# One more couple by seven products, a weight combination made on the fly, and an input tile sent alone

## The chip, the cores and the metric

The kernel runs on one core of a Trainium2 chip. The metric is the device time of one execution in microseconds (us); smaller is better. A kernel is run several times and the median is given, with the lowest and highest run beside it. One execution of each kernel is also recorded by the hardware profiler; its span is the time from the first to the last instruction recorded.

The engines of the core are TensorE (PE in the profile: matrix products into the PSUM banks; PEld is its weight load), VectorE (DVE), ScalarE (ACT), GpSimd (POOL) and SyncE (SP), which here issues most transfers (DMAs). Each engine runs its own instructions in order and waits for the others by semaphores.

## The reference

A trunk of two layers on 256 tokens of width 2048, all in fp32. Each layer has a token mixer (mLSTM in the first, HGRN2 in the second) and a gated feed-forward part, both added to the stream; a norm closes it. What matters here is the feed-forward part, and of it the second product:

```python
def conv_glu(hn, w_up, conv_w, conv_b, w_down):
    u = hn @ w_up
    a, v = jnp.split(u, 2, axis=-1)
    ...
    return (jax.nn.gelu(c, approximate=False) * v) @ w_down

for layer in range(DEPTH):
    ...
    h = h + mix
    h = h + conv_glu(rmsnorm(h, norm_ffn_g[layer]), ffn_w_up[layer], ...)
return rmsnorm(h, final_g)
```

`w_down` is 5504 x 2048 in each layer.

## The kernel before

**Products.** Each fp32 operand is split into a high part (rounded, for PE) and a low part (what is left). A product of two operands is three matmuls: high x high, high x low, low x high. `product` (L236) issues the three. For weights, `parts` (L141 to L149) makes the split: ACT casts the high part `wh` (L147), DVE subtracts and leaves `wl` (L148). This is done for every piece of 128x1024 or 128x512 numbers that PE uses, just ahead of it; six pieces can be in flight.

**Stages.** A list of chunks runs through PE one after the other: the mLSTM mixer, the feed-forward of layer 0, the HGRN2 mixer, the feed-forward of layer 1. A feed-forward part is worked in two halves of its 5504 inner columns, 22 and 21 tiles of 128. Each half first computes its up tiles (each ended by `done_up`, from L1187: the gate, the convolution and the product, which leaves the tile `g` in its two parts), then multiplies them with the down weights in two pairs: output columns 0 to 1023, then 1024 to 2047. "The last half" below is the second half of layer 1, with 21 tiles; "the first pair" and "the last pair" are its two pairs. Their results are added to the stream `hm` in `done` (L598) and, in the last pair, in the final norm's `half` (L505 to L532), which works on 128 tokens at a time.

**Units.** In a pair, two inner tiles make a unit (or couple); the last half has units 0 to 10, the last of one tile. A unit is a product of 2 x 2 blocks. The plain way has eight block products (24 matmuls of 512 columns). The units that `SEVEN` names are done with seven (21 matmuls), by the scheme of Strassen in Winograd's form: it needs four sums of token blocks (`token_sums`, L561 to L573, made in `done_up` when the second tile of a unit is there, and kept in tiles `sx`) and four combinations of weight blocks (T1 to T4). A plain unit has two pieces of weights to split, each 128x1024. A unit of seven has four: two from `raw` and two from T (128x1024 and 128x512). Its sums stand in four banks of their own (P1, P6, P7, P5) beside the four of the result (C11, C12, C21, C22), and `mid` (L581 to L592) adds them to the stream at the last unit of seven, half on DVE (L585 to L590) and half on POOL (L591, L592).

**Where the weight combinations come from.** Either beforehand: `prepare` (L608 to L637), during the up tiles, loads the blocks (`praw`), makes four subtractions on DVE (L632) and stores them in DRAM (`tscr`, L635); `raw(u)` (L185 to L193) loads them back later, 768 KB as T (L198) and 256 KB into `raw` (L199). Or on the fly, for the units in `FLY`: `combine` (L195 to L209) makes four subtractions of 128x512 on DVE (L207) from the loaded weights one unit ahead. Before the change the entry of the last half is empty: all of its units are prepared, as twelve of 1 MB items in the last half's up tiles.

**The end.** The last three units of the last pair are handled by `ending` (L252 to L277), which orders the products by token half, so that the norm of the first 128 tokens runs beside the products of the second. The second half's last bank is split in two of 256 columns (`rest`).

**The start.** The first chunk's weights come as sixteen transfers of 256 KB (L707) and its input as tiles of 128 KB: the first two on ACT's queue, then pairs of tiles (256 KB, L717) on SP's queue, each ahead of its two weights. ACT and DVE split each x tile (L379, L380), and L147/L148 the weights; the products are L373.

**What sets the order.** The instructions are placed by a scheduler that simulates the engines, in the order in which data is expected. Some calls are pinned to the program's order (`pin`), such as the ending's products and the start's transfers. The side work of `prepare` is spread evenly over the up tiles by a period (`prep`). Each transfer goes out in queue order on its engine.

Of the kernel before, what the change touches and what calls it, by code (L numbers as in the profile page):

```python
# [8 lines left out]
F32 = mybir.dt.float32  # L9
# [6 lines left out]
P = 128  # L16
# [32 lines left out]
GATES = 4 * AH  # L49
SEVEN = ((1, 2, 3, 4, 5, 6, 7, 8, 9), (1, 2, 3, 4, 5, 6, 7, 8)), ((1, 2, 3, 4, 5, 6, 7, 8, 9), (1, 2, 3, 4, 5, 6, 7))  # L50
FLY = (2,), (5,), (2,), ()
FIRST = 6
# [14 lines left out]
def trunk_kernel(ctx, tc, xT, x_d, fg_d, pp_d, cst_d, w_gate, w_first, w_aq, w_ak, w_av, w_ao, w_aout, w_ao2,  # L67
# [70 lines left out]
    def split_weights(chunks):  # L138
# [14 lines left out]
        for k in range(KT):  # L153
            for i in range(k, k + 2 if k else 1) if k % 2 == 0 else ():
                first.x(i, pin)
            wh, wl = parts(raws[k], 512, pin)
            if k == 1:
                first.x(1, pin)
            yield wh, wl, 1
# [65 lines left out]
    def squares_by_seven(ch, fetch, ready):  # L225
# [19 lines left out]
        def ending(u0):  # L245
            while len(ready) < ch.nk - 2 * u0:
                fetch()
            for t in range(2):
                c, todo, left = (C11, C12, C21, C22)[2 * t:2 * t + 2], [], iter(ready)
                for k in range(2 * u0, ch.nk, 2):  # L250
                    p, x0 = next(left)[:2], half(ch.x(k), t)
                    todo += [(0, x0, block(p, 0))]  # L252
                    if k + 1 == ch.nk:
                        todo += [(1, x0, block(p, 1))]
                        break
                    q, x1 = next(left)[:2], half(ch.x(k + 1), t)
                    todo += [(1, x1, block(p, 1)), (0, x1, block(q, 0)), (1, x0, block(q, 1))]
                if t:
                    todo.sort(key=lambda o: o[0])
                end = [max(i for i, o in enumerate(todo) if o[0] == j) for j in range(2)]  # L260
                tail = [o for o in todo if o[0]] if t else []
                for i, (j, x, w) in enumerate(todo[:len(todo) - len(tail)]):
                    product(c[j], x, w, i == end[j], pin)
                if t:
                    rest, n = psm.tile([P, 512], F32, tag="mm", name="rest"), len(tail) - 1
                    for i, (_, x, w) in enumerate(tail):
                        product(c[1][:, 0:256], x, [v[:, 0:256] for v in w], i == n, pin, id(c[1]))
                    for i, (_, x, w) in enumerate(tail):
                        product(rest[:, 0:256], x, [v[:, 256:512] for v in w], i == n, pin, id(rest))
                    c = (*c, rest)  # L270
                ch.half(c, t)

# [203 lines left out]
    class FinalNorm:  # L476
# [27 lines left out]

        def half(self, ps, t):  # L505
            side.drain()
# [5 lines left out]
            h = hm[:, t, 1536:2048]  # L512
            dve.tensor_tensor(h, h, ps[1], ALU.add)
            m = 256 if t else 512
# [45 lines left out]

    def token_sums(mp, i, a, b, S, last=None):  # L561

        m = 384 if last else 512
        sx = mp.tile([P, 2 * m], F32R, tag=f"sx{i}", name="sx")
        for i, (x, y, op) in enumerate(((a[:, P:T], b[:, P:T], ALU.add), (a[:, P:T], a[:, 0:P], ALU.subtract),
                                        (S[:, 0:P], a[:, 0:P], ALU.subtract), (b[:, 0:P], S[:, 2 * P:3 * P], ALU.subtract))):
            dve.tensor_tensor(S[:, i * P:(i + 1) * P], x, y, op)
        act.copy(sx[:, 0:m], S[:, 0:m])
        dve.tensor_tensor(sx[:, m:2 * m], S[:, 0:m], sx[:, 0:m].bitcast(F32), ALU.subtract)
        if last:  # L570
            act.copy(last[0], S[:, m:512])
            dve.tensor_tensor(last[1], S[:, m:512], last[0].bitcast(F32), ALU.subtract)
        return [(sx[:, i * P:(i + 1) * P], sx[:, m + i * P:m + (i + 1) * P]) for i in range(m // P)] + ([last] if last else [])  # L573

# [114 lines left out]
    def mlstm(norm, nxt):  # L689
# [12 lines left out]
        def load(loaded, follower):  # L702
# [3 lines left out]
            def w(k):  # L706
                pin(nc.sync.dma_start(raws[k], w_first[:, k * 512:(k + 1) * 512]))  # L707
# [7 lines left out]
            w(1)  # L715
            for k in range(2, KT, 2):
                pin(nc.sync.dma_start(gx[:, KT + k * T:KT + (k + 2) * T], xT[:, KT + k * T:KT + (k + 2) * T]))  # L717
                w(k)
                w(k + 1)
            late(wg, w_gate)  # L720
# [454 lines left out]
    def ffn(layer, norm, nxt):  # L1175
# [13 lines left out]
        def done_up(f, i, GT, SX, seven):  # L1189
            def go(ps):  # L1190
# [18 lines left out]
                if i % 2 and i // 2 in seven:  # L1209
                    n = seven.index(i // 2)  # L1210
                    z = GT[i - 1][:, P:T], GT[i - 1][:, T + P:2 * T]
                    SX[i // 2] = token_sums(mp, n, box["c"], c, avc[:, 0:2 * T], z)
                box["c"] = c
            return go

        for part, (f0, nf) in enumerate(((0, FA), (FA, FB))):
# [29 lines left out]
            seven, fly = SEVEN[layer][part], FLY[2 * layer + part]  # L1246
            n = len(seven) - len(fly)
            chunks.append(two(w0, 0, nxt if part else None, seven, fly, (0, 0, n) if part else (FIRST, n - FIRST)))
            chunks.append(two(w1, 2, nxt if part and not ending else None, seven, fly, SPLIT[layer] if part else (0, n)))
            if part:  # L1250
# [132 lines left out]
```

## Time and profile before

| | us |
|---|---|
| median of 3 runs | 2368.31 |
| lowest and highest run | 2367.0, 2369.95 |
| the profiled execution, its own time | 2366.48 |
| its span | 2364.5 |
| PE busy in it | 2354.1 |
| first pair of the last half, PE's first start | 2250.33 |
| last pair, PE's first start | 2303.87 |
| PE's last matmul | 2356.30 |

In the rows of a timeline the columns are: start in us from the span's beginning, duration, engine, line, operation, what it writes and reads, shape, and how many were merged into the row. A bracket gives how long the engine stood idle before it and what released it. `SPq` rows are transfers being issued. Matmul rows overlap, so the pace of PE is read from starts. In the view of waits the three numbers are the total in us, the times and the longest. In a table of windows the columns after the stretch are its length, busy us and instructions of PE, PEld, DVE, ACT and POOL, the granted clock of PE as a share of full speed, the share in which the DMA engines were busy, and GB/s moved.

### The profile page before, as it was taken

What the parts mean: (1) busy time and instruction counts of PE and PEld (TensorE: products, weight loads), DVE (VectorE), ACT (ScalarE), POOL (GpSimd) and SP (SyncE); (2) the same over time, 40 slices, a digit from 0 to 9 for tenths busy, and PEclk for the clock granted to TensorE, in tenths of its full rate; (3) what the DMA queues carried; (4) which work ended last, traced back from release to release, by engine and by line L of the source; (5) the groups of instructions that cost most, each with busy time, mean ns of one, the idle gap of its engine ahead of it and who ended that gap; (6) DMA issues with size and microseconds to landing.
All of it is one profiled execution on the core that took longest, in us unless ns stands there. A gap on an engine that the chain in (4) does not pass through costs nothing. (4 is left out here: it accounts for less than half of the span.)

```text
span 2364.5 us, 38407 instructions
## 1 busy us (share of the span) xinstructions
PE 2354.1 (100%) x14545; PEld 2016.2 (85%) x14545; DVE 1993.5 (84%) x3087; ACT 1470.0 (62%) x2340; POOL 196.5 (8%) x244
## 2 busy tenths in 40 slices
PE   9999999999999999999999999999999999999998
PEld 8888888888888888888888888888888888888887
DVE  7777687888998898897888888778789889888888
ACT  7655456555665555676777777776555567455565
POOL 0100000000000000000232322220000000000000
PEclk9999999999999999999999999999999999999999
DMA  8776656888888878996556665646788888888896
GB/s 303 239 248 242 213 195 211 295 282 292 313 321 327 306 282 292 330 334 230 208 203 223 212 225 204 214 169 228 270 300 289 289 321 335 295 287 302 309 351 221
DMA packets 122266, 632.97 MB, mean 268 GB/s; under 512 B 13776, under 2 KB 14928, under 8 KB 77664
## 3 DMA queue, kind: packets, MB, share of 16 engines
q1 hardware_dynamic: 120384, 626.51, 75.0%
q0 software_dynamic: 1120, 3.21, 0.8%
q8 instruction: 114, 1.87, 0.3%
q10 hardware_dynamic: 576, 0.79, 0.1%
q14 instruction: 72, 0.59, 0.1%
HBM read 562.24 MB, written 68.22 MB: 267 GB/s over the span
## 5 line engine op out<-in xcount | busy, mean ns | idle before, releaser
L357 PE MATMUL mm<-xt,wh 128*128 128x512 f32 x3776 | 1312.0, 394 | 0.0
L148 DVE TENSOR_TENSOR wl<-raw,wh 128x1024 fp32r<-128x1024 f32 (+1 forms) x844 | 1037.3, 1234 | 222.6 <-ACT wh L147 214.5
L147 ACT CAST wh<-raw 128x1024 fp32r<-128x1024 f32 (+1 forms) x844 | 875.3, 1042 | 513.0 <-PE mm L357 305.8
L361 PE MATMUL mm<-xt,wl 128*128 128x256 f32 x3776 | 1043.5, 278 | 0.0
L357 PEld LDWEIGHTS mm<-xt,wh 128*128 128x128 f32 x3776 | 705.6, 188 | 160.6 <-issue 0.4
L361 PEld LDWEIGHTS mm<-xt,wl 128*128 128x128 f32 x3776 | 709.4, 188 | 4.5
L373 PE MATMUL mm<-wh,xt 128*128 128x512 f32 x1024 | 324.4, 392 | 0.6 <-ACT wh L147 0.5
L236 PE MATMUL pc<-wh,g 128*128 128x512 f32 (+1 forms) x716 | 243.2, 388 | 0.3 <-ACT wh L147 0.2
L373 PEld LDWEIGHTS mm<-wh,xt 128*128 128x128 f32 x1024 | 191.2, 188 | 40.0 <-ACT wh L147 1.1
L632 DVE TENSOR_TENSOR praw<-praw 128x512 f32<-128x512 f32 x252 | 174.1, 691 | 44.7 <-DMA praw<-in_w_d 29.0
L373 PE MATMUL mm<-wl,xt 128*128 128x512 f32 x512 | 199.7, 391 | 0.0
L236 PEld LDWEIGHTS pc<-wh,g 128*128 128x128 f32 x716 | 134.1, 188 | 29.0 <-ACT wh L147 1.5
L236 PE MATMUL mm<-wh,sx 128*128 128x512 f32 x432 | 153.4, 389 | 0.0
L148 DVE TENSOR_TENSOR wl<-T,wh 128x1024 fp32r<-128x1024 f32 (+1 forms) x144 | 135.9, 955 | 13.3 <-ACT wh L147 8.9
L147 ACT CAST wh<-T 128x1024 fp32r<-128x1024 f32 (+1 forms) x144 | 118.6, 835 | 44.7 <-DMA T<-tscr 18.2
L236 PE MATMUL pc<-wl,g 128*128 128x512 f32 (+1 forms) x358 | 138.8, 388 | 0.0
L591 POOL TENSOR_TENSOR hm<-hm,u 128x512 f32<-128x512 f32 x10 | 14.8, 1481 | 1223.8 <-DVE u L590 1223.8
L373 PEld LDWEIGHTS mm<-wl,xt 128*128 128x128 f32 x512 | 96.2, 188 | 18.6
L1071 DVE TENSOR_TENSOR QK<-QK,G 128x256 f32<-128x256 f32 x224 | 104.6, 515 | 6.2 <-ACT kq L1050 5.9
L1195 ACT COPY avc<-mm 128x256 f32<-128x256 f32 x172 | 64.0, 372 | 63.9 <-PE mm L361 63.6
L1050 ACT COPY kq<-QK 128x512 f32<-128x512 f32 x112 | 74.5, 669 | 37.3 <-DVE QK L1071 29.5
L236 PEld LDWEIGHTS mm<-wh,sx 128*128 128x128 f32 x432 | 81.0, 188 | 16.9 <-ACT wh L147 0.2
(246 smaller groups left out, 2263.1 us busy)
## 6 DMA issues: line engine op xcount, KB each, us to landing
raw<-in_w_up SPq DMA_DIRECT2D x172, 1024.0 KB, 6.1
tscr<-praw SPq DMA_DIRECT2D x126, 512.0 KB, 6.7
praw<-in_w_d SPq DMA_DIRECT2D x120, 512.0 KB, 6.8
raw<-in_w_bq SPq DMA_DIRECT2D x48, 1024.0 KB, 5.0
T<-tscr SPq DMA_DIRECT2D x63, 768.0 KB, 7.6
raw<-in_w_d SPq DMA_DIRECT2D x60, 768.0 KB, 6.0
raw<-in_w_ao SPq DMA_DIRECT2D x24, 1024.0 KB, 4.8
raw<-in_w_d SPq DMA_DIRECT2D x24, 1024.0 KB, 7.7
```

Source lines behind the costliest of these rows:

```text
L147: pin(act.copy(wh[:, :m], r))
L148: pin(dve.tensor_tensor(wl[:, :m], r, wh[:, :m].bitcast(F32), ALU.subtract))
L236: pin(pe.matmul(ps, a, b, start=bank not in begun, stop=stop and i == 2))
L357: hold(pe.matmul(ps[f], wh[:, c:c + P], x, start=k + kk == 0, stop=False))
L361: hold(pe.matmul(ps[f][:, 0:T], wl[:, c:c + P], x[:, 0:T], start=False, stop=k + kk == ch.nk - 1))
L373: pe.matmul(ps[t], x[:, a + t * P:a + (t + 1) * P], w[:, c], start=st and i == 0, stop=sp and i == 2)
L591: pool.tensor_tensor(part(1, 0), part(1, 0), u, ALU.add)
L632: dve.tensor_tensor(out, x, y, ALU.subtract)
L1050: act.copy(m, blocks(QK, h))
L1071: dve.tensor_tensor(two[:, j], two[:, j], by[:, j], ALU.mult)
L1195: act.copy(z, p[:, T:2 * T])
```

## The change

It has four parts. (1) `SEVEN` gets unit 0 in the last half, but for the last pair alone (`each`): there unit 0 is done with seven products. Its token sums are kept in two tiles of their own, so that they need no place in `z`, the token block that the other units overwrite. (2) `FLY` names unit 2 for the last half: in both its pairs T of unit 2 is combined on DVE from the loaded weights; eleven items are prepared instead of twelve. (3) In the ending, the first addition of the second token half's last bank covers 256 columns where 512 stood (`wide`). (4) At the start, x tiles 2 and 3 are sent as two transfers of 128 KB, tile 3 behind the weights of step 2.

```diff
--- before.py
+++ after.py
@@ -47,8 +47,8 @@
 LEAD = 48
 TEMP = 3
 GATES = 4 * AH
-SEVEN = ((1, 2, 3, 4, 5, 6, 7, 8, 9), (1, 2, 3, 4, 5, 6, 7, 8)), ((1, 2, 3, 4, 5, 6, 7, 8, 9), (1, 2, 3, 4, 5, 6, 7))
-FLY = (2,), (5,), (2,), ()
+SEVEN = ((1, 2, 3, 4, 5, 6, 7, 8, 9), (1, 2, 3, 4, 5, 6, 7, 8)), ((1, 2, 3, 4, 5, 6, 7, 8, 9), (0, 1, 2, 3, 4, 5, 6, 7))
+FLY = (2,), (5,), (2,), (2,)
 FIRST = 6
 SPLIT = (0, 2, 5), (0, 2, 5)
 END = 3
@@ -151,7 +151,7 @@
         first, loaded = chunks[0], []
         raws = first.load(loaded, chunks[1])
         for k in range(KT):
-            for i in range(k, k + 2 if k else 1) if k % 2 == 0 else ():
+            for i in (k,) if k in (0, 2, 3) else (k, k + 1) if k % 2 == 0 else ():
                 first.x(i, pin)
             wh, wl = parts(raws[k], 512, pin)
             if k == 1:
@@ -261,14 +261,16 @@
                 tail = [o for o in todo if o[0]] if t else []
                 for i, (j, x, w) in enumerate(todo[:len(todo) - len(tail)]):
                     product(c[j], x, w, i == end[j], pin)
+                wide = 512
                 if t:
+                    wide = 512 if id(c[1]) in begun else 256
                     rest, n = psm.tile([P, 512], F32, tag="mm", name="rest"), len(tail) - 1
                     for i, (_, x, w) in enumerate(tail):
                         product(c[1][:, 0:256], x, [v[:, 0:256] for v in w], i == n, pin, id(c[1]))
                     for i, (_, x, w) in enumerate(tail):
                         product(rest[:, 0:256], x, [v[:, 256:512] for v in w], i == n, pin, id(rest))
                     c = (*c, rest)
-                ch.half(c, t)
+                ch.half(c, t, wide)
 
         units, last = (ch.nk + 1) // 2, max(ch.seven)
         for u in range(units):
@@ -502,7 +504,7 @@
                 dve.tensor_tensor(ss[:, :, 0:1], ss[:, :, 0:1], ss[:, :, 1:2], ALU.add)
                 dve.tensor_scalar(self.rc, ss[:, :, 0], 1.0 / D, EPS, ALU.mult, ALU.add)
 
-        def half(self, ps, t):
+        def half(self, ps, t, wide):
             side.drain()
             ss, rc = self.ss[:, t], self.rc[:, t:t + 1]
             dve.tensor_tensor(hm[:, t, 1024:1536], hm[:, t, 1024:1536], ps[0], ALU.add)
@@ -510,7 +512,7 @@
             dve.tensor_scalar(rc, ss[:, 2:3], 1.0 / D, rc, ALU.mult, ALU.add)
             last = keep.tile([P, 512], F32, tag=f"xt{4 + t}", name="fl")
             h = hm[:, t, 1536:2048]
-            dve.tensor_tensor(h, h, ps[1], ALU.add)
+            dve.tensor_tensor(h[:, 0:wide], h[:, 0:wide], ps[1][:, 0:wide], ALU.add)
             m = 256 if t else 512
             dve.scalar_tensor_tensor(last[:, 0:m], h[:, 0:m], 1.0 / D, h[:, 0:m], ALU.mult, ALU.mult, accum_out=ss[:, 3:4])
             dve.tensor_tensor(rc, rc, ss[:, 3:4], ALU.add)
@@ -558,19 +560,22 @@
         return where.tile([P, 2 * T], F32R, tag=f"yt{j}", name=f"{name}{j}")
 
 
-    def token_sums(mp, i, a, b, S, last=None):
+    def token_sums(mp, i, a, b, S, last=None, to=None):
 
         m = 384 if last else 512
-        sx = mp.tile([P, 2 * m], F32R, tag=f"sx{i}", name="sx")
+        if to is None:
+            sx = mp.tile([P, 2 * m], F32R, tag=f"sx{i}", name="sx")
+            to = sx[:, 0:m], sx[:, m:2 * m]
+        hi, lo = to
         for i, (x, y, op) in enumerate(((a[:, P:T], b[:, P:T], ALU.add), (a[:, P:T], a[:, 0:P], ALU.subtract),
                                         (S[:, 0:P], a[:, 0:P], ALU.subtract), (b[:, 0:P], S[:, 2 * P:3 * P], ALU.subtract))):
             dve.tensor_tensor(S[:, i * P:(i + 1) * P], x, y, op)
-        act.copy(sx[:, 0:m], S[:, 0:m])
-        dve.tensor_tensor(sx[:, m:2 * m], S[:, 0:m], sx[:, 0:m].bitcast(F32), ALU.subtract)
+        act.copy(hi, S[:, 0:m])
+        dve.tensor_tensor(lo, S[:, 0:m], hi.bitcast(F32), ALU.subtract)
         if last:
             act.copy(last[0], S[:, m:512])
             dve.tensor_tensor(last[1], S[:, m:512], last[0].bitcast(F32), ALU.subtract)
-        return [(sx[:, i * P:(i + 1) * P], sx[:, m + i * P:m + (i + 1) * P]) for i in range(m // P)] + ([last] if last else [])
+        return [(hi[:, i * P:(i + 1) * P], lo[:, i * P:(i + 1) * P]) for i in range(m // P)] + ([last] if last else [])
 
     def pair(src, nk, c0, x, sums, norm, seven):
 
@@ -713,10 +718,10 @@
             x(nc.scalar, KT + T, KT + 2 * T)
             w(0)
             w(1)
-            for k in range(2, KT, 2):
-                pin(nc.sync.dma_start(gx[:, KT + k * T:KT + (k + 2) * T], xT[:, KT + k * T:KT + (k + 2) * T]))
-                w(k)
-                w(k + 1)
+            for k, n in [(2, 1), (3, 1)] + [(k, 2) for k in range(4, KT, 2)]:
+                pin(nc.sync.dma_start(gx[:, KT + k * T:KT + (k + n) * T], xT[:, KT + k * T:KT + (k + n) * T]))
+                for j in range(n):
+                    w(k + j)
             late(wg, w_gate)
             for b in (0, 2048):
                 r = wpool.tile([P, 2048], F32, tag="raw", bufs=RAW, name="raw")
@@ -1207,9 +1212,12 @@
                 dve.tensor_tensor(g[:, T:2 * T], c, g[:, 0:T].bitcast(F32), ALU.subtract)
                 GT.append(g)
                 if i % 2 and i // 2 in seven:
-                    n = seven.index(i // 2)
-                    z = GT[i - 1][:, P:T], GT[i - 1][:, T + P:2 * T]
-                    SX[i // 2] = token_sums(mp, n, box["c"], c, avc[:, 0:2 * T], z)
+                    n = seven.index(i // 2) - (seven[0] == 0)
+                    z, to = (GT[i - 1][:, P:T], GT[i - 1][:, T + P:2 * T]), None
+                    if n < 0:
+                        z, to = None, [mp.tile([P, 768], F32R, tag=f"sx{len(seven) - 1 + j}", name="sx")[:, 0:2 * T]
+                                       for j in range(2)]
+                    SX[i // 2] = token_sums(mp, n, box["c"], c, avc[:, 0:2 * T], z, to)
                 box["c"] = c
             return go
 
@@ -1244,9 +1252,10 @@
 
             w0, w1 = w_d0[layer][:, f0 * 1024:(f0 + nf) * 1024], w_d3[layer] if part else w_d1[layer]
             seven, fly = SEVEN[layer][part], FLY[2 * layer + part]
-            n = len(seven) - len(fly)
-            chunks.append(two(w0, 0, nxt if part else None, seven, fly, (0, 0, n) if part else (FIRST, n - FIRST)))
-            chunks.append(two(w1, 2, nxt if part and not ending else None, seven, fly, SPLIT[layer] if part else (0, n)))
+            each = [u for u in seven if u], seven
+            n = len(each[0]) - len(fly)
+            chunks.append(two(w0, 0, nxt if part else None, each[0], fly, (0, 0, n) if part else (FIRST, n - FIRST)))
+            chunks.append(two(w1, 2, nxt if part and not ending else None, each[1], fly, SPLIT[layer] if part else (0, n)))
             if part:
                 chunks[-1].last = ending
                 if ending:
```

The scheduler's order stays as it was up to the last half's up tiles, except for the four transfers at the start.

SP's queue at the end of the last half's up tiles, from the last transfers of up weights on (`raw<-in_w_d` are down weights, 128x1536 for a prepared unit of seven, 128x2048 otherwise); before:

```order
L395 DMA raw<-in_w_up 128x2048
L635 DMA tscr<-praw 128x1024 x2
L135 DMA raw<-in_w_d 128x2048
L635 DMA tscr<-praw 128x1024
L135 DMA raw<-in_w_d 128x1536
L199 DMA raw<-tscr 128x512
L635 DMA tscr<-praw 128x1024
L198 DMA T<-tscr 128x1536
```

and after:

```order
L397 DMA raw<-in_w_up 128x2048 x2
L397 DMA praw<-in_w_d 128x1024 x2
L135 DMA raw<-in_w_d 128x2048
L135 DMA raw<-in_w_d 128x1536
L199 DMA raw<-tscr 128x512
L640 DMA tscr<-praw 128x1024 x2
L198 DMA T<-tscr 128x1536
L135 DMA raw<-in_w_d 128x2048
```

T here is unit 1's, in the first pair. Behind it the next unit's load, which was 128x1536 with a T of its own, is now 128x2048.

DVE around the end of the first pair (L598 before and L603 after are the additions of its result, L498 and L500 the norm's factor; rows `wl<-T` belong to units of seven of the last pair); before:

```order
L590 TENSOR_TENSOR u<-u,mm 128x512
L148 TENSOR_TENSOR wl<-raw,wh 128x1024 x3
L598 TENSOR_TENSOR hm<-hm,pc 128x512
L148 TENSOR_TENSOR wl<-raw,wh 128x1024
L598 TENSOR_TENSOR hm<-hm,pc 128x512 x2
L148 TENSOR_TENSOR wl<-raw,wh 128x1024
L598 TENSOR_TENSOR hm<-hm,pc 128x512
L148 TENSOR_TENSOR wl<-T,wh 128x1024
L148 TENSOR_TENSOR wl<-raw,wh 128x1024
```

and after:

```order
L595 TENSOR_TENSOR u<-u,mm 128x512
L148 TENSOR_TENSOR wl<-raw,wh 128x1024 x3
L148 TENSOR_TENSOR wl<-T,wh 128x1024
L148 TENSOR_TENSOR wl<-raw,wh 128x1024 x3
L603 TENSOR_TENSOR hm<-hm,pc 128x512
L148 TENSOR_TENSOR wl<-T,wh 128x512
L603 TENSOR_TENSOR hm<-hm,pc 128x512
L207 TENSOR_TENSOR T<-raw 128x512
L603 TENSOR_TENSOR hm<-hm,pc 128x512 x2
L500 TENSOR_TENSOR hm<-hm,fg_23048 128x512
L148 TENSOR_TENSOR wl<-T,wh 128x1024
L207 TENSOR_TENSOR raw<-raw 128x512
```

Seven pieces now stand between the middle additions of the first pair and its last ones, where three stood; unit 0's `wl<-T` is among them, and the combination of unit 2 (L207) among the additions.

DVE at the ending of the last pair (L585 to L589 before are L590 to L594 after: the additions of the seven-product sums; the pieces are those of units 8 and 9); before:

```order
L148 TENSOR_TENSOR wl<-raw,wh 128x1024 x2
L585 TENSOR_TENSOR hm<-hm,mm 128x512
L586 TENSOR_TENSOR u<-u,mm 128x512
L148 TENSOR_TENSOR wl<-raw,wh 128x1024
L587 TENSOR_TENSOR hm<-hm,mm 128x512
L589 TENSOR_TENSOR hm<-hm,mm 128x512
L148 TENSOR_TENSOR wl<-raw,wh 128x1024 x2
```

and after:

```order
L148 TENSOR_TENSOR wl<-raw,wh 128x1024 x3
L592 TENSOR_TENSOR hm<-hm,mm 128x512
L594 TENSOR_TENSOR hm<-hm,mm 128x512
L590 TENSOR_TENSOR hm<-hm,mm 128x512
L591 TENSOR_TENSOR u<-u,mm 128x512
L148 TENSOR_TENSOR wl<-raw,wh 128x1024 x2
```

The four additions, which stood in two groups of two with a piece between, now stand together.

## The prediction

> **What bounds the kernel now.** I began with the page's head, to see which engine has no room.
>
> ```profile
> span 2364.5 us, 38407 instructions
> PE 2354.1 (100%) x14545; PEld 2016.2 (85%) x14545; DVE 1993.5 (84%) x3087; ACT 1470.0 (62%) x2340; POOL 196.5 (8%) x244
> ```
>
> TensorE (PE) is busy for 2354.1 of 2364.5 us. Time can be won in two ways only: fewer matmuls, or PE's few idle stretches. The view of waits, for PE, lists these.
>
> ```profile
> PE idle L1266 <- POOL ones L1259: 1.1, 1, 1.1
> PE mm L236 <- DVE wl L148: 0.5, 1, 0.5
> PE mm L373 <- ACT wh L147: 0.5, 2, 0.3
> PE pc L236 <- ACT wh L147: 0.2, 1, 0.2
> ```
>
> Beyond the wait of 1.1 us at the program's start, PE waits for 1.2 us in all. So no edit here can win much from waits, and one that makes PE wait loses at once. But this view counts only the time in which PE ran nothing; matmuls overlap, so the loss of a stall is read better from starts. The timeline of PE at the start of the first pair of the last half, units 1 and 2:
>
> ```profile
> 2256.68 0.39 PE L236 MATMUL pc<-wl,g 128*128 128x512 f32 x1
> ...
> 2260.31 0.39 PE L236 MATMUL pc<-wh,g 128*128 128x512 f32 x1
> 2260.86 0.40 PE L236 MATMUL pc<-wh,g 128*128 128x512 f32 x1
> 2261.79 0.50 PE L236 MATMUL mm<-wl,g 128*128 128x512 f32 x1 [0.53 <-DVE wl L148]
> ...
> 2263.73 0.39 PE L236 MATMUL mm<-wh,sx 128*128 128x512 f32 x1
> ```
>
> Between the first two rows lie 16 starts in 3.63 us: a matmul of 512 columns costs 0.227 us. Between 2260.31 and 2263.73 lie 10 starts, which should take 2.27 us and took 3.42. The stall at unit 2 cost 1.15 us, of which the view of waits shows 0.5.
>
> Who made it? VectorE (DVE) had the low part of unit 2's first piece late. Its rows, ScalarE's (ACT) and the queue's:
>
> ```profile
> 2239.59 0.42 SPq L198 DMA_DIRECT2D T<-tscr  x1
> 2251.58 1.05 ACT L147 CAST wh<-T 128x1024 fp32r<-128x1024 f32 x1 [3.04 <-DMA T<-tscr]
> 2252.66 1.23 DVE L148 TENSOR_TENSOR wl<-T,wh 128x1024 fp32r<-128x1024 f32 x1 [3.16 <-DMA raw<-tscr]
> 2260.51 1.23 DVE L148 TENSOR_TENSOR wl<-raw,wh 128x1024 fp32r<-128x1024 f32 x1 [0.51 <-ACT wh L147]
> DMA to landing us min/median/max: 5.9/7.7/11.9
> 2240.00:2246.00 6.00, 6.00 (x36) 5.26 (x36) 4.65 (x9) 3.44 (x5) 2.21 (x4) 1.00 0.92 308
> 2246.00:2252.00 6.00, 6.00 (x34) 5.15 (x34) 3.46 (x5) 2.38 (x4) 0.00 (x0) 1.00 1.03 414
> 2252.00:2258.00 6.00, 6.00 (x28) 4.99 (x27) 4.66 (x7) 3.54 (x7) 0.00 (x0) 1.00 0.80 285
> ```
>
> Unit 1's combined weights T were asked for at 2239.59 and landed 11.9 us later (the longest of the landing line), under a DMA share of 0.92 to 1.03 (last column but one). Both engines stood for 3 us before them, and since each runs in order, the last up tile's work and unit 2's pieces came late in turn.
>
> **The change part by part.** *Fewer products.* Unit 0 of the very last pair takes seven products for eight. A product is three matmuls, so three starts fall away: 3 x 0.227 = **-0.68 us**. The first pair keeps its eight there.
>
> *The late T.* With unit 2 combined on DVE, the last prepared item (1 MB read, 1 MB written) is gone from the up stage, and unit 2's T load with it; in the new order of the queue T of unit 1 has less ahead of it. 2 MB at the 308 GB/s of the window are 6.5 us of traffic, more than the 3 us by which T was late. In exchange DVE makes four subtractions in the first pair before unit 2's T piece. Their length has a row of the same helper in other halves, and their pitch a row of three like them:
>
> ```profile
> L207 DVE TENSOR_TENSOR T<-raw x18: 677/686/693, 320.8 to 1973.2; 128x512 f32<-128x512 f32 x18
> 2310.41 1.88 DVE L498 TENSOR_TENSOR hm<-hm,fg 128x512 f32<-128x512 f32 x3
> ```
>
> (1.88 - 0.68) / 2 = 0.60 us each, 2.4 together. In the windows 2246 to 2258 above DVE is busy 3.46 and 4.66 of 6 us, so 3.88 us are free and cover them. I take the whole stall as gone: **-1.15**. Ends: -1.15, and +1.25 if T is as late as before and the 2.4 us come on top (2.4 - 1.15).
>
> *The last pair.* Unit 0 now has two pieces more (128x1024 and 128x512), and unit 2's combination stands among the additions that end the pair before (three of the four ahead of unit 2's first piece). DVE there, and the matmul that needs that piece:
>
> ```profile
> 2302.26 0.69 DVE L598 TENSOR_TENSOR hm<-hm,pc 128x512 f32<-128x512 f32 x1 [2.69 <-PE pc L236]
> 2306.93 1.22 DVE L148 TENSOR_TENSOR wl<-T,wh 128x1024 fp32r<-128x1024 f32 x1
> 2308.07 1.22 DVE L148 TENSOR_TENSOR wl<-raw,wh 128x1024 fp32r<-128x1024 f32 x1
> 2309.80 0.68 DVE L148 TENSOR_TENSOR wl<-T,wh 128x512 fp32r<-128x512 f32 x1
> 2312.28 1.22 DVE L148 TENSOR_TENSOR wl<-raw,wh 128x1024 fp32r<-128x1024 f32 x1
> 2314.07 0.39 PE L236 MATMUL mm<-wh,g 128*128 128x512 f32 x1
> ```
>
> By pitches the additions are 1.14 (2306.93 to 2308.07) + 0.61 (2309.80 to 2310.41) + 2.40 = 4.15 us. From 2302.26 on DVE has no gap; unit 2's first piece, begun at 2312.28, is ready 1.14 later at 2313.42, 0.65 us before its matmul, which moreover comes 0.68 earlier now. Against that stands the idle 2.69 us ahead of 2302.26: the new order has seven pieces between the last of the middle additions and the first of these, where three stood, and the four more can fill it. 4.15 + 0.68 - 0.65 - 2.69 = 1.49 us, if all of it has to be done before that matmul. The fourth subtraction (0.60) stands behind unit 2's first piece, and some of the pieces ahead of that one are for later products; I take half, **+0.75**. Ends: 0, and 4.18 if nothing fills the idle time (raw weights not landed, or no free buffer). ACT's two more casts (1.05 and 0.62) lie in its idle time.
>
> *The ending.* Before, the sums of the seven products were added in two groups, with unit 9's first piece between them; now all four additions stand ahead of it.
>
> ```profile
> 2342.18 1.22 DVE L148 TENSOR_TENSOR wl<-raw,wh 128x1024 fp32r<-128x1024 f32 x1
> 2343.31 0.68 DVE L587 TENSOR_TENSOR hm<-hm,mm 128x512 f32<-128x512 f32 x1
> ```
>
> From the start of the last product's last matmul: 0.39 for it, some 0.1 to hand over, 4 x 0.60, 1.22 for the piece: 4.1 us. PE has 16 matmuls before it needs that piece, 16 x 0.227 = 3.63. That is **+0.45** (ends 0 and +1.0, if the additions wait for the product before too).
>
> *The start.* The third x tile no longer waits for the fourth's bytes, and the weights of step 2 go out before the fourth.
>
> ```profile
> 1.64 0.42 SPq L717 DMA_DIRECT2D gx<-in_xT  x1
> 2.11 0.91 SPq L707 DMA_DIRECT2D raw<-in_w_first  x2
> 8.34 0.39 PE L373 MATMUL mm<-wh,xt 128*128 128x512 f32 x1
> 8.34 1.30 ACT L147 CAST wh<-raw 128x512 fp32r<-128x512 f32 x2 [1.06 <-DMA raw<-in_w_first]
> 9.01 1.21 PE L373 MATMUL mm<-wh,xt 128*128 128x512 f32 x4 [0.29 <-ACT wh L147]
> 10.06 0.62 PE L373 MATMUL mm<-wl,xt 128*128 128x512 f32 x2
> ```
>
> PE loses 9.01 - 8.34 - 0.227 = 0.44 and 10.06 - 9.01 - 4 x 0.227 = 0.14 us here, since ACT had no weights until 8.34. 128 KB less ahead of them are 0.31 us at the 414 GB/s shown above: **-0.3**. Ends: -0.58 (the stall), and +0.4, one more issue on SP (2.11 - 1.64 = 0.47) in front of the weights that follow, if these have no slack; a step is 12 matmuls, 2.7 us, so I think they have.
>
> The Trainium skill, "DMA: Bandwidth & Descriptors", section Bandwidth, asks for transfers of 1 MiB and more, and gives 0.95 us for 64 KB and 6.15 for 1 MB; read between, as an estimate, 256 KB are 2.0 us and 128 KB are 1.3. By it the weights gain 0.7 us and the whole 0.58 would go (sum lower by 0.28), while two pieces together cost 0.6 more than one for all that comes behind.
>
> *Edits at nothing.* Two: the sums of unit 0's tokens in the second up tile (four of at most the 256-column row's 0.42, one of 0.68, 2.4 us together), for DVE's row of that stage is
>
> ```profile
> 2040.00:2062.00 22.00, 22.00 (x129) 19.22 (x128) 17.98 (x27) 11.55 (x19) 0.00 (x0) 1.00 0.96 346
> 2355.03 0.68 DVE L513 TENSOR_TENSOR hm<-hm,pc 128x512 f32<-128x512 f32 x1
> 2356.62 0.42 DVE L519 TENSOR_TENSOR hm<-hm,rest 128x256 f32<-128x256 f32 x1 [0.25 <-PE rest L236]
> ```
>
> 17.98 of 22 us busy, and one prepared item less. Without that cover it would be +2.4 at most. The second is the halved addition in the norm: 0.68 - 0.42 = 0.26 saved, but DVE then waits 0.25 for PE's `rest` anyway. It can win at most 0.26.
>
> **Sum:** -0.68 - 1.15 + 0.75 + 0.45 - 0.30 = -0.93. The span goes from 2364.5 to 2363.6; the profiled run took 2366.48, 1.83 less than the median of 2368.31, and the difference goes onto the median: **2367.4 us**.
>
> **The rivals.** (A) *The last pair starves.* DVE's pieces of unit 0 cannot be made in the idle 2.69 us, and PE waits 4.18 us in units 1 to 3: -0.93 - 0.75 + 4.18 = +2.5, **2370.8**, slower. It decides once more than 1.7 of the 2.69 us stay unfilled (0.93 + 0.75 of room). For it: DVE has no gap from 2302.26 to past the matmul at 2314.07. Against it: three raw buffers let the loads run ahead of the pieces.
>
> (B) *The first pair's stall stays*, because the four subtractions take the place of the late T: +0.22 with the stall as it is, **2368.5**, up to 2370.9 with the 2.4 us on top. For it: DVE's order holds three of them among the last up tile's work. Against it: 3.88 us of idle time.
>
> (C) *The split tile costs.* +0.4 for -0.3: **2368.1**. For it the issue time on SP; against it the 2.7 us of a step.
>
> (D) *No new stall:* DVE gets by in the last pair and at the ending, and the start's stall goes whole: -0.68 - 1.15 - 0.58 = -2.41, **2365.9**.
>
> **How the numbers follow.** The forecast 0.45, A 0.18, B 0.14, C 0.06, D 0.17. The cases lie between 2365.9 and 2370.9. The runs of before alone differ by 2.95 us (2367.0 to 2369.95), so a median can be off by about 1 us; the range of 2365.0 to 2370.8 holds the forecast, C, D, most of B and half of A, and the likeliest case alone has 2366 to 2369. About 0.2% (4.7 us) is what a measurement of this kernel can tell from no change: faster means under 2363.6, slower over 2373.0. No case reaches either by itself: faster needs D and a shift of 2.3 us, slower needs A and the late end of B together. That gives 0.05, 0.87 and 0.08.
>
> **What would show it.** Right: the page counts some three matmuls fewer than 14545, and near the first pair's unit 2 no start is late by over 0.3 us; in the last pair's units 1 to 3 the starts lose 0.5 to 1 us to `wl`; at unit 9 about 0.4; the lateness at 8.34 us is about half. Wrong: a T of unit 1 landing as late as before, a first subtraction of the last pair's unit 0 that begins only after 2302, or starts delayed by over 1.5 us in one unit. A span changed by more than 3 us either way would say that something moved that this sum does not hold, most likely in the chunks before the last half, which I take to run as they did.

## The result, and the profile after

| | before | after |
|---|---|---|
| median of 22 runs each, us | 2368.22 | 2372.03 |
| lowest and highest run | 2365.69, 2369.95 | 2367.79, 2376.59 |
| span of the profiled execution | 2364.5 | 2368.3 |
| PE's last matmul begins | 2356.30 | 2359.79 |

The ratio is 1.0018, with a 95% interval of 1.0012 to 1.0024: slower by 3.8 us, where 0.9 us less was forecast; 2372.03 lies beyond the range (2370.8). The runs also scatter twice as widely as before. The head of the page of the changed kernel, and its view of waits for PE:

```profile
span 2368.3 us, 38400 instructions
PE 2354.8 (99%) x14542; PEld 2016.0 (85%) x14542; DVE 1998.9 (84%) x3098; ACT 1472.5 (62%) x2343; POOL 194.4 (8%) x244
PE pc L236 <- DVE wl L148: 1.9, 1, 1.9
PE mm L236 <- ACT wh L147: 1.6, 3, 1.2
PE idle L1275 <- POOL ones L1268: 1.1, 1, 1.1
PE pc L236 <- ACT wh L147: 0.2, 1, 0.2
```

Three matmuls went, as counted. The old wait of 0.5 us is gone, and new ones of 1.9 and 1.6 us (three together, the longest 1.2) are there. Where they lie, the timeline of PE shows: in the last pair near unit 2, and at unit 9 in the ending.

```profile
2311.97 0.39 PE L236 MATMUL pc<-wh,g 128*128 128x512 f32 x1
2312.57 0.50 PE L236 MATMUL mm<-wh,g 128*128 128x512 f32 x1 [0.21 <-ACT wh L147]
2312.91 0.40 PE L236 MATMUL pc<-wh,g 128*128 128x512 f32 x1
2314.55 0.73 PE L236 MATMUL mm<-wh,sx 128*128 128x512 f32 x2 [1.25 <-ACT wh L147]
2315.12 0.40 PE L236 MATMUL pc<-wl,g 128*128 128x512 f32 x1
...
2346.41 0.61 PE L236 MATMUL pc<-wh,g 128*128 128x512 f32 x2
2348.91 0.50 PE L236 MATMUL pc<-wl,g 128*128 128x512 f32 x1 [1.89 <-DVE wl L148]
```

From 2311.97 to 2315.12 there are 5 starts (a row x2 holds two), 1.14 us at 0.227; they took 3.15, so 2.0 us are lost. From 2346.41 two starts should take 0.45 and took 2.50: 2.05 lost, and 0.11 at the next. All told, in us:

| place | lost before | lost after | forecast of the difference |
|---|---|---|---|
| the three matmuls | | | -0.68 |
| start, step 0 | 0.20 | 0.56 | 0 |
| start, step 2 | 0.58 | 0 | -0.30 |
| first pair, unit 2 | 1.15 | 0 | -1.15 |
| first pair, unit 4 | 0 | 0.93 | 0 |
| last pair, near unit 2 | 0 | 2.0 | +0.75 |
| ending, unit 9 | 0 | 2.15 | +0.45 |

The differences with the three matmuls give +3.0, and PE's first product began 0.15 us earlier (5.45 against 5.60): +2.9. PE's end moved by 3.49 and the span by 3.8. Of what is left, 0.3 arose in chunks before the last half, where nothing was changed, 0.3 after the last matmul, and the rest in gaps of about 0.1 us each.

Who made PE wait near unit 2: DVE's and ACT's rows there.

```profile
2306.06 0.69 DVE L207 TENSOR_TENSOR T<-raw 128x512 f32<-128x512 f32 x1 [0.95 <-DMA raw<-in_w_d]
2309.60 0.69 DVE L207 TENSOR_TENSOR raw<-raw 128x512 f32<-128x512 f32 x1
2310.20 0.68 DVE L148 TENSOR_TENSOR wl<-T,wh 128x512 fp32r<-128x512 f32 x1
2310.81 1.89 DVE L500 TENSOR_TENSOR hm<-hm,fg 128x512 f32<-128x512 f32 x3
2312.68 0.68 DVE L207 TENSOR_TENSOR T<-raw 128x512 f32<-128x512 f32 x1
2307.44 0.63 ACT L538 ACTIVATE jk<-hm 128x512 f32<-128x512 f32 x1 [0.95 <-DVE hm L603]
2309.58 2.93 ACT L147 CAST wh<-raw 128x1024 fp32r<-128x1024 f32 x3
2313.45 2.00 ACT L147 CAST wh<-T 128x1024 fp32r<-128x1024 f32 x2 [0.94 <-DVE T L207]
```

The 2.0 us have two parts. The larger, 1.5 us (the gap that ends at 2314.55 and 0.1 at the next start), hangs on T. PE waits for its high part, which ACT casts as soon as DVE's third subtraction is done (2312.68 to 2313.36). That one stands behind three multiplications by the norm's factors (L500, 1.89 us), for which nobody waits before the kernel's end. The smaller, 0.5 us (at 2312.57), hangs on the raw weights. The first subtraction waits 0.95 us for them (2306.06), two additions behind it come late, so do the squares that ACT makes of their results (2307.44), and with these the three casts of raw pieces (2309.58), the last of which is unit 2's first piece.

The same at unit 9:

```profile
2343.02 1.05 ACT L147 CAST wh<-raw 128x1024 fp32r<-128x1024 f32 x1 [1.62 <-DMA raw<-in_w_d]
2344.45 2.00 ACT L147 CAST wh<-raw 128x1024 fp32r<-128x1024 f32 x2
2344.11 1.23 DVE L148 TENSOR_TENSOR wl<-raw,wh 128x1024 fp32r<-128x1024 f32 x1 [1.26 <-ACT wh L147]
2345.25 0.68 DVE L592 TENSOR_TENSOR hm<-hm,mm 128x512 f32<-128x512 f32 x1
2347.04 0.68 DVE L591 TENSOR_TENSOR u<-u,mm 128x512 f32<-128x512 f32 x1
2347.64 2.36 DVE L148 TENSOR_TENSOR wl<-raw,wh 128x1024 fp32r<-128x1024 f32 x2
```

Which pieces these are, the instruction order says, with the numbers of the tiles:

```
L148 TENSOR_TENSOR wl_23862<-raw_23842,wh_23861 128x1024
L592 TENSOR_TENSOR hm_75<-hm_75,mm_23499 128x512
...
L148 TENSOR_TENSOR wl_23845<-raw_23842,wh_23844 128x1024
```

Both come from unit 9's weights, and PE uses 23845 first. So the piece at 2343.02 and 2344.11 is unit 9's *second*; the *first* one is subtracted at 2347.64, behind four additions (2345.25 to 2347.64). So two things meet: the weights landed at 2343, and of two pieces DVE took the one that PE needs later.

### The profile page after: what moved, and what is told of

It reads as the page before. It is cut to its first block, busy times and chain, and to the rows that moved or that the text cites. A ratio compares the mean times of both kernels' runs of the same rounds, so it can differ in the third digit from the quotient of the medians.

```text
span 2368.3 us, 38400 instructions
## 1 busy us (share of the span) xinstructions
PE 2354.8 (99%) x14542; PEld 2016.0 (85%) x14542; DVE 1998.9 (84%) x3098; ACT 1472.5 (62%) x2343; POOL 194.4 (8%) x244
```

## The experiments

Each ran beside the kernel before on the same chip, but not all on the same one. The median of before was 2366.3 to 2366.7 there, so ratios and profiles are compared, and medians only where before's is the same. "Lost" is read from starts as above; units 2 and 9 are those of the last pair.

| run | ratio to before (95% interval) | median / before beside it | lost near unit 2 | lost at unit 9 | lost in the first pair |
|---|---|---|---|---|---|
| on the fly in the first pair only | 1.0002 (0.9993 to 1.0011) | 2368.16 / 2366.44 | 0 | 0 | 2.8 |
| no seven in unit 0 | 0.9999 (0.9990 to 1.0008) | 2366.54 / 2366.44 | 0 | 0.56 | 0 |
| one piece ahead of the additions | 1.0025 (1.0016 to 1.0034) | 2372.69 / 2366.44 | 1.24 | 4.35, at its second piece | 0 |
| what seemed to help | 1.0000 (0.9992 to 1.0009) | 2366.84 / 2366.44 | 0 | 0 | 1.9 |
| DVE loaded by repetition | 0.9999 (0.9990 to 1.0007) | 2366.20 / 2366.62 | 0 | 1.08 | 0 |
| both pieces ahead | 1.0007 (0.9998 to 1.0016) | 2369.51 / 2366.62 | 1.11 | 0 | 0.79 |
| x tiles together | 1.0010 (1.0001 to 1.0019) | 2369.32 / 2366.62 | 0.56 | 2.03 | 1.11 |
| the change again | 1.0014 (1.0005 to 1.0023) | 2370.34 / 2366.62 | 1.29 | 1.51 | 0.43 |
| factors held back | 1.0006 (0.9997 to 1.0015) | 2367.22 / 2366.28 | 0 | 0.31 | 0.28 |
| the same again | 1.0004 (0.9995 to 1.0013) | 2367.13 / 2366.74 | 0.41 | 0.35 | 0.41 |
| one item earlier | 1.0034 (1.0021 to 1.0046) | 2375.79 / 2366.28 | 0 | 0.91 | 0 |
| two on the fly | 0.9996 (0.9987 to 1.0005) | 2365.69 / 2366.74 | 0 | 1.0 | 0 |

**On the fly in the first pair only.** `FLY` is given by pair; the last pair's unit 2 is prepared again (one item more).

```diff
+FLY0, FLY1 = (2,), ()                   # first pair, last pair
-SPLIT = (0, 2, 5), (0, 2, 5)
+SPLIT = (0, 2, 5), (0, 2, 6)
...
```

> The change, but unit 2 of the last pair is prepared again (combined on the fly in the first pair alone). Theory D (DVE's four subtractions in the last pair stand in its order behind the additions that end the first pair, and the lag that they leave makes unit 9's raw weights late): the 1.42 + 0.37 us stalls near unit 2 of the last pair go, unit 9's stall falls from 2.05 to about 0.45, span 2368.3 - 2.0 - 1.6 = 2364.7. Rival P (the two more pieces of unit 0, 1.75 us on DVE, do it): a stall of 1 us or more stays in units 0 to 3 of the last pair, unit 9's stays near 2, span 2367 or more.

Both stalls of the last pair are gone, as theory D had it, though unit 0 keeps its seven products and its two pieces; rival P falls. The saving is spent in the first pair, where T again came late at two places, so the span was 2366.8 where D had 2364.7.

**No seven in unit 0.**

```diff
-SEVEN = ..., (..., (0, 1, 2, 3, 4, 5, 6, 7))
+SEVEN = ..., (..., (1, 2, 3, 4, 5, 6, 7))
-SPLIT = (0, 2, 5), (0, 2, 5)
+SPLIT = (0, 2, 5), (0, 2, 4)
```

> The change without its first part: unit 0 of the last pair by eight products again (three matmuls more, +0.68 us; ten items prepared). Theory D: the stall of over 1 us near unit 2 of the last pair stays, since the combination still stands there; unit 9's falls by what a lag of 1.75 us less gives, 0.5 to 1.6; span 2367.4 to 2368.5. Rival P: both stalls go, span 2368.3 + 0.7 - 2.0 - 1.6 = 2365.4.

D expected the stall near unit 2 to stay, since the combination still stands there. It went. So neither part alone makes it. This run's DVE timeline:

```profile
2302.59 0.69 DVE L207 TENSOR_TENSOR T<-raw 128x512 f32<-128x512 f32 x1 [1.20 <-DMA raw<-in_w_d]
...
2309.06 0.69 DVE L207 TENSOR_TENSOR T<-raw 128x512 f32<-128x512 f32 x1
2309.66 1.89 DVE L500 TENSOR_TENSOR hm<-hm,fg 128x512 f32<-128x512 f32 x3
```

The third subtraction is *ahead* of the three multiplications here, 3.6 us earlier than in the change. That left two readings: too much work in all, or its order.

**DVE loaded by repetition.** The run above, with 1.74 us of useless work for DVE at unit 0's first piece, which leaves the kernel's output as it is.

```diff
+for b in again:                         # (1024, 512) at unit 0's first piece of the last pair, else nothing
+    dve.tensor_tensor(wl[:, :b], r[:, :b], wh[:, :b].bitcast(F32), ALU.subtract)
```

> The kernel without the first part (unit 0 of the last pair by eight products, unit 2 on the fly in both pairs), but DVE repeats two subtractions on unit 0's first piece of the last pair, one of 128x1024 and one of 128x512 (1.74 us by pitch, as much as unit 0's T pieces take on DVE; nothing else is loaded or cast). Theory Sum (either load alone fits into DVE's idle time there, the two together don't): a stall of 0.8 us or more near unit 2 of the last pair is back, and unit 9's is over 1 us; median 2 to 4 us over before. Rival Q (it is T's loads and its buffers, three of them, that hold up the queue, not DVE's time): no stall over 0.5 us at units 0 to 3 of the last pair, median as without the repetition.

Theory Sum falls for the stall near unit 2: DVE did 1.74 us more in the same place, and nothing was lost there. At unit 9 it lost 1.08 us where the run above lost 0.56, but the median stayed level with before. In its order too the subtractions stand ahead of the multiplications. It came out as rival Q had it, but what Q names, T's loads, was not tried here.

**Factors held back.** The change, with the order of DVE set by hand in the last pair.

```diff
-yield 3.0
+yield 18.0                              # FinalNorm.scale: the factors later
-dve.tensor_tensor(hm[:, t, cs], hm[:, t, cs], self.g[c], ALU.mult)
+pin(dve.tensor_tensor(hm[:, t, cs], hm[:, t, cs], self.g[c], ALU.mult))
...
+hold = pin if ch.last else lambda ins: ins
-dve.tensor_tensor(out, x, y, ALU.subtract)
+hold(dve.tensor_tensor(out, x, y, ALU.subtract))
```

> The change with one order altered in the last pair: the four multiplications by the norm's factors (2.4 us on DVE, needed by nobody before the end) are held back behind unit 2's four subtractions, which keep their own order. All loads, pieces and sums are those of the change; at the ending the additions stand in two groups again, with unit 9's first piece between. Theory O (the order on DVE: the third subtraction, for which ACT's cast of T waits, stands behind work that could wait): no stall over 0.4 us near unit 2 of the last pair, unit 9's under 0.6, median 2.5 to 4 us below the change's, at or just under before. Rival L (the late landing of unit 2's raw weights, for which the first subtraction waited 0.56 and 0.95 us, sets the stall): 1 us or more stays near unit 2.

Its view of waits for PE, and rows of DVE and ACT:

```profile
PE mm L376 <- ACT wh L147: 0.4, 1, 0.4
PE pc L237 <- ACT wh L147: 0.4, 2, 0.2
PE mm L237 <- ACT wh L147: 0.3, 1, 0.3
...
2305.53 0.69 DVE L208 TENSOR_TENSOR T<-raw 128x512 f32<-128x512 f32 x1 [0.49 <-DMA raw<-in_w_d]
2308.47 0.68 DVE L208 TENSOR_TENSOR raw<-raw 128x512 f32<-128x512 f32 x1
2309.75 0.69 DVE L208 TENSOR_TENSOR T<-raw 128x512 f32<-128x512 f32 x1
...
2318.14 2.00 ACT L147 CAST wh<-raw 128x1024 fp32r<-128x1024 f32 x2 [2.77 <-DMA raw<-in_w_d]
```

Theory O holds for the larger part. Loads, pieces and sums are those of the change, the raw weights of unit 2 are late here too (the first subtraction waits 0.49 us for them, against 0.95 and 0.56 in the two profiles of the change), and the third subtraction is done 2.9 us earlier: no stall near unit 2. At unit 3 a new 0.45 us is lost, since raw weights come late there (2318.14). At unit 9, where the order changed along with it, 0.31 is lost. Rival L falls as the whole cause, and Q of the run before with it: the two issues of T, the second of which waits for a buffer, take about as long with the stall (the change, first row) as without it (this run):

```profile
2304.54 6.70 SPq L198 DMA_DIRECT2D T<-tscr  x2
```

```profile
2304.48 5.63 SPq L198 DMA_DIRECT2D T<-tscr  x2
```

> The run with the factors held back once more, for a second profile and eleven more times. Theory O: no stall over 0.5 us near unit 2 of the last pair or at unit 9 in this profile either, and the median within 1 us of before. If the first profile was a lucky one, a stall of 1 us is back at one of the two places.

The second profile lost 0.41 near unit 2 and 0.35 at unit 9, within what was expected, but 0.89 at unit 3, which was not. Its raw weights for unit 2 were as late as in the first profile of the change:

```profile
2305.40 0.69 DVE L208 TENSOR_TENSOR T<-raw 128x512 f32<-128x512 f32 x1 [0.92 <-DMA raw<-in_w_d]
```

So a part of rival L stays: a wait of 0.92 or 0.95 us for these weights came with 0.4 to 0.5 us lost near unit 2 in either order, one of 0.49 or 0.56 with none of it. The rest of the stall came and went with the order alone. Both medians are level with before (both intervals hold 1), 0.9 and 0.4 us above it. Against the change's 1.0018 and 1.0014 the four intervals overlap one by one. Taken together, and weighted by their widths (an estimate), they give 1.0017 for the change and 1.0005 with the factors held back, 0.0012 apart with an interval of about 0.0008 either way.

**One piece ahead of the additions**, and **both pieces ahead**: the additions of the ending are pinned behind unit 9's first piece, and then behind both.

```diff
+hold = pin if ch.last and u >= units - END else lambda ins: ins
-yield *parts(r[:, 0:1024], 1024, more=ch.pool), 1
+yield *parts(r[:, 0:1024], 1024, hold, more=ch.pool), 1
...
+hold(dve.tensor_tensor(part(0, 0), part(0, 0), P1, ALU.add))   # and the others of mid
```

> The change with one order altered: at the ending, the additions of the seven-product sums are pinned behind the split of unit 9's first piece. Theory M (unit 9's stall is the 2.4 us of four additions ahead of that piece): raw weights land near 2343, cast by 2345.5, subtracted by 2346.7, and PE needs them at 2346.9: stall under 0.3, span 2368.3 - 2.0 = 2366.3. Rival W (the weights' late landing, 1.62 us of ACT's idle time, is what PE waits for): stall of 1.5 us or more stays, span 2367.8 or more.

> The change with one order altered: both pieces of unit 9 are pinned ahead of the four additions at the ending, unit 10's piece behind them. Theory M (the order ahead of unit 9's pieces makes the stall there): with weights that land as in the change, unit 9 waits under 0.4 us, unit 10 at most 0.5, and the median is 1.5 to 2 us below the change's; the stall near unit 2 stays. Rival W (weights that land 1.6 us later than before are the cause): unit 9 waits 1.2 us or more still.

With one piece ahead the stall did not go, as M had expected, and the span was 2368.8 where M had 2366.3. It moved: unit 9's first piece was ready (2343.26 + 1.22), and PE waited for the second, which the pins had put behind six additions:

```profile
2343.26 1.22 DVE L148 TENSOR_TENSOR wl<-raw,wh 128x1024 fp32r<-128x1024 f32 x1 [2.43 <-ACT wh L147]
2344.40 0.68 DVE L592 TENSOR_TENSOR hm<-hm,mm 128x512 f32<-128x512 f32 x1
2347.52 0.68 DVE L597 TENSOR_TENSOR u<-u,mm 128x512 f32<-128x512 f32 x1
2348.11 1.22 DVE L148 TENSOR_TENSOR wl<-raw,wh 128x1024 fp32r<-128x1024 f32 x1
...
2349.39 0.80 PE L237 MATMUL pc<-wl,g 128*128 128x512 f32 x1 [2.68 <-DVE wl L148]
```

With both ahead, unit 9 loses nothing and unit 10 0.40. The median fell by 0.8 us against the change beside it (2370.34), where 1.5 to 2 was expected. M's mechanism holds in both, though its figure for the first did not: whichever piece stands behind the additions stalls PE. Rival W falls as the whole cause; in the second profile of the change too, unit 9 lost 1.51 though its weights held ACT up by only 0.47 us:

```profile
2341.26 1.05 ACT L147 CAST wh<-raw 128x1024 fp32r<-128x1024 f32 x1 [0.47 <-DMA raw<-in_w_d]
```

**The start.** The change without its fourth part, and the change once more.

> The change without its fourth part: x tiles 2 and 3 in one transfer again. Theory X (the separate tile brings the weights of step 2 forward by about 0.3 us): the stall at step 2, 0.2 to 0.6 us in the profiles with separate tiles, is 0.5 to 0.8 here. Rival N (it does nothing that can be told from the scatter of transfers; four profiles with the tiles apart showed 0.20, 0.73, 0.54 and 1.15): within 0.2 to 1.2 as well. The rest as in the change.

> The changed kernel once more, for a second profile. If the three stalls found in its first profile belong to the kernel (1.9 us near unit 2 and 2.05 at unit 9 of the last pair, 0.9 near unit 4 of the first pair), each is within 0.7 us of that here too; the one that moves more is chance of the transfers. Median 3 to 5 us over before.

With the tiles together step 2 lost 1.59 us here and 0.58 in the profile before; with the tiles apart twelve profiles lost from 0 to 1.26 there. (The 0.20 that the expectation gives for the first of them lies at step 0; at step 2 it lost nothing.) The twelve fall into two groups. In four, the weights of step 2 landed at 6.5 to 6.7 us and step 2 lost nothing; in the other eight they landed at 8.2 to 8.8, as with the tiles together (8.3 and 8.9). So the split did not bring the weights forward by a steady 0.3 us, and with two profiles of the one and twelve of the other, whether it is what brings the early landings is not settled. The second profile of the change has all three stalls, 1.29, 1.51 and 0.43: smaller each, in the same places.

**What seemed to help.** The change with eight products in unit 0 and the last pair's unit 2 prepared.

> Only what seemed to help: unit 2 of the first pair on the fly, the x tiles apart, the narrower addition; unit 0 of the last pair by eight products, its unit 2 prepared. Theory D: no stall over 0.5 us in the last pair, the first pair's unit 2 without its 1.15; span 2364.5 - 1.15 - 0.36 = 2363.0, the ratio to before 0.9994. Rival F (the first pair gives its gain back at unit 4, where T now lands late, 0.93): span 2363.9 or more with that stall in the trace.

Rival F came true: no stall in the last pair, but 1.9 us lost in the first one, at 2271.5, where T is late. In the change the same place shows it:

```profile
2270.57 1.05 ACT L147 CAST wh<-T 128x1024 fp32r<-128x1024 f32 x1 [4.46 <-DMA T<-tscr]
```

**One item earlier**, and **two on the fly**: two ways to ten prepared items in the last half, both with the factors held back.

```diff
-SPLIT = (0, 2, 5), (0, 2, 5)            # one item earlier
+SPLIT = (0, 2, 5), (0, 3, 4)
...
+FLY0, FLY1 = (2, 5), (2,)               # two on the fly: first pair, last pair
```

> As the run with the factors held back, but one of the prepared items is moved from the last half's up tiles to the first half's (ten there for eleven, as in the two kernels with unit 0 by eight products, which showed no stall in the first pair). Theory T (with less traffic at the end of the up tiles, the first pair's T land in time): the 0.4 to 0.9 us near unit 4 of the first pair go, and the median is 0.5 to 1 us below the run with the factors held back. Rival U (that stall is the queue's order, T of unit 4 behind raw weights that wait for a buffer): it stays, the two medians agree within 0.5.

> The run with the factors held back, with unit 5 of the first pair on the fly too: ten prepared items in the last half's up tiles, and the first half's stay as they were; DVE makes four more subtractions in the first pair. Theory T (less traffic at the end of the up tiles brings the first pair's T in time): no stall over 0.3 us near unit 4 of the first pair; nothing new at units 5 to 7, since DVE has idle time ahead of the last pair; median 0.5 to 1 us below the kernel with the factors held back. Rival V (the four subtractions at unit 5 make DVE late for unit 6 or the last pair's first units): stalls over 0.5 us there, median level or above.

With ten items the first pair lost nothing in either (nor in the two runs above that have ten); with eleven it lost from 0 to 1.9 us in eight profiles, with twelve 1.15 (before) and 2.8. Theory T holds there. But the item that was moved cost far more where it went, in the up tiles of the first half. The view of waits for PE, and DVE there:

```profile
PE mm L364 <- DVE wl L148: 6.7, 5, 2.2
...
1813.25 0.69 DVE L638 TENSOR_TENSOR praw<-praw 128x512 f32<-128x512 f32 x1 [4.64 <-DMA praw<-in_w_d]
```

DVE waited in its order for an item's load, and PE for the pieces behind it: 9.6 us by that stage's end. Two on the fly has no such cost. Rival V's stalls at units 5 to 7 did not come; 1.0 is lost at unit 9. The profiled execution was the longest of its eleven runs (2369.0 us) and has a wait of 2.2 us at 1029 us, in layer 0, where nothing was changed. The median is 1.05 us below before beside it, but the interval holds 1: a version that beats before is not shown.

## Why the prediction was wrong

- **The three matmuls**: right, x14545 to x14542.
- **The late T of the first pair**: unit 2's stall went, as said. ACT's cast of unit 1's T began at 2249.44, 2.1 us earlier than before, less than the 6.5 us of traffic that were taken out. The step left out what is late next: T of unit 4, 0.93 and 0.43 us in two profiles. The queue was read only up to unit 1's T.
- **The last pair** is the step that failed first. It summed DVE's work (4.15 us) against its idle time (2.69) and asked only when unit 2's first piece is ready. The seven pieces did fill the idle time (DVE has no gap from 2298.62 to 2305.11), and it can carry more still (the repetition). What PE waited for was another instruction, the third subtraction, and its place behind the factors; +0.75 became +2.0 and +1.29, and the matmuls waited for the high parts that ACT casts, not for `wl`, as the prediction's sign had it. That place stands in the instruction order; the part of it on which the prediction rested ends at the second subtraction, ahead of the three factors. Of the +2.0, 0.5 is something else that the step had at nothing, the late landing of unit 2's raw weights.
- **The ending**: the mechanism was right, four additions ahead of a piece of unit 9. The size was not: +0.45 became +2.15 and +1.51. The step took the piece ahead of the additions for one that is in time; it was unit 9's second piece, which waits for weights that landed at 2343, so the additions began late, and the first piece came last.
- **The start**: -0.3 is not shown. In the first profile step 2 lost nothing, but step 0 lost 0.36 us more, and the stall at step 2 went in four of twelve profiles only. The case against rival C rested on a step of 12 matmuls; the starts from 9.01 to 10.52 are six, so a step is 1.36 us, still longer than the 0.47 of the issue.
- **The rivals**: A named the right place and side and nearly the sum (2.5 us against the 3.8 measured), but its mechanism, DVE short of time there, is what the repetition ruled out. The chance of 0.18 for it was low for a change whose added work on DVE fell into a stretch without a gap. The prediction's sign for a span off by over 3 us pointed at the chunks before the last half; they gave 0.3. Its 0.87 for a time within 0.2% of before came true (0.18%), but by another sum.

The slower time is thus for the most part the scheduler's order on DVE in two places. Near unit 2, 1.5 of the 2.0 us went in two profiles when the third subtraction was set ahead of the factors by hand; at unit 9 the 2.15 went in one profile when both pieces were set ahead of the additions. With all of the change's work kept and the factors held back (which also puts the ending's additions in two groups again), the ratio falls from 1.0018 and 1.0014 to 1.0006 and 1.0004, level with before.

What remains open: whether the weights of unit 9 land later because of the stall near unit 2 or for another reason, and why the change gives no gain even with its order mended. Its terms say -0.7, which runs of this scatter cannot tell. The stalls that stay in the last half (first pair, units 2, 3 and 9 of the last) sum to 1.0 and 2.1 us in the two profiles with the factors held back, against 1.15 before, so in the second of them 0.9 us of the gain are spent there.

## What to carry to other kernels

Count not only whether an engine has time for added work, but which instruction each waiter needs, and what stands ahead of that instruction in its engine's order; read the order to the end of the stretch. Work that nobody waits for (norm factors, sums into the residual) belongs behind the piece that feeds the matmuls, and where a scheduler places by readiness it has to be pinned there. Where gains are under 0.1%, one profile's stall at a transfer may be chance: here the late T of unit 4 cost the same kernel 0.93 us in one profile and 0.43 in the next.

## What the runs showed of the hardware

PE lost more than its wait when the wait was long. In the run with one piece ahead, PE waited 2.68 us; in the windows around it the granted clock (last column but two) is 0.51 behind the wait:

```profile
2340.00:2346.00 6.00, 6.00 (x28) 4.99 (x27) 3.57 (x5) 3.54 (x4) 0.00 (x0) 1.00 0.15 62
2346.00:2349.00 3.00, 0.70 (x4) 0.24 (x2) 2.96 (x5) 0.00 (x0) 0.72 (x1) 1.00 0.01 3
2349.00:2352.40 3.40, 3.01 (x7) 2.43 (x8) 2.55 (x2) 0.00 (x0) 3.40 (x2) 0.51 0.00 0
2352.40:2356.00 3.60, 3.60 (x17) 2.91 (x17) 2.36 (x6) 0.72 (x2) 0.79 (x2) 0.99 0.02 5
```

From 2349.39 on, 7 starts took 3.12 us for 1.59: 1.5 us on top of a stall of 2.85. The changed kernel's wait of 1.89 us left the clock at 1.00:

```profile
2348.90:2352.00 3.10, 3.09 (x13) 2.55 (x14) 2.38 (x3) 0.00 (x0) 0.60 (x1) 1.00 0.02 5
```

In between, the length alone did not decide it: in the run with one item earlier, the clock stayed at 1.00 in the 3.4 us after a wait of 2.24 us (ended at 1816.13) and was 0.72 in the 3.4 us after one of 2.20 us (ended at 1888.16). The Trainium skill, "TensorE: Matmul & The Clock Gate", Part 1, puts the drop after an idle stretch of about 3.4 us; here 2.68 us were enough.
